# A hybrid decoder layer: the attention values as seven block products instead of two plain passes

## The chip, the cores and the metric

The kernel runs on one core of a Trainium2 chip. The metric is the device time of one execution in microseconds (us), as a median over runs. Engines are named TensorE (PE, with PEld for its weight loads), VectorE (DVE), ScalarE (ACT), GpSimd (POOL) and SyncE (SP); SP, ACT and POOL also issue DMA transfers, each from a queue of its own that runs in order.

## The reference

One decoder layer, float32, 512 tokens, width 1024:

```python
x = x + 0.5 * swiglu(rms_norm(x, norm_ffn1_w), ffn1_w_in, ffn1_w_out)
x = x + hybrid_mixer(rms_norm(x, norm_mix_w), w_in_mix, ..., rel_bias, w_out_mix, lambda_init)
x = x + memory_cross_attention(rms_norm(x, norm_cross_w), rms_norm(mem, norm_mem_w), ...)
x = x + 0.5 * swiglu(rms_norm(x, norm_ffn2_w), ffn2_w_in, ffn2_w_out)
return rms_norm(x, norm_final_w)

def hybrid_mixer(h, w_in, ...):
    z, xbc, dt_raw, q, k, v = split_sizes(h @ w_in, IN_SIZES)
    # state-space group: conv, silu, 16 heads in 4 groups, scan in chunks of 128 tokens,
    # gate by silu(z), group norm  ->  y_ssd
    # differential attention: 8 heads, two softmaxes a head,
    #   w = p[:, :, 0] - lam * p[:, :, 1];  o = w @ v;  norm by head  ->  y_attn
    return concatenate([y_ssd, y_attn], axis=-1) @ w_out
```

The change concerns `v = h @ w_in[:, 5136:6160]`, a product of 512 x 1024 by 1024 x 1024, and some steps that lie round it in time.

## The kernel before, in words

**Tiles.** Activations lie with features on the 128 partitions and the 512 tokens along the row: eight tiles `x[k]` of 128 x 512. Products in nearly full float32 precision are made of fast float32r matmuls: every operand is split into a high part (rounded by ScalarE, L155) and a low part (the rest, by VectorE, L156), and a product is three matmuls, high by high, high by low, low by high (`mm3`, L312). `load_w` (L172) brings a weight tile of 128 x 1024 from memory on SP's queue and splits it; six such tiles can be raw (`wr`), three split (`wh`, `wl`).

**Block products.** The feed-forwards use Winograd's form of Strassen's method: both operands are cut into 2 x 2 blocks, and seven products of sums of blocks replace eight products. `quad` (L257) does that with weights stationary and 256 tokens streaming; `out_blocks` (L1158) does it with activations stationary and 512 weight columns streaming ("by token"). Sums of activation blocks are made by VectorE (`sums_of`, L199: four sums of 256 columns, then a split into high and low); sums of weight blocks come from transfers that add into SBUF, issued on POOL's queue (`raw_w`, L243), from VectorE (L294, L297), or, for the second feed-forward, from sums that are made in DRAM ahead of time by `block_sums_in_dram` (L1138), a chain that issues one copy on SP and one adding transfer on POOL for each of some 46 tiles.

**Order.** `Order` (L57) writes the program down. Dense work (`od.add`) is a list of generators, taken one after the other; beside it run chains (`od.spawn`), each of which says after every step how many microseconds of TensorE time are to pass until its next one. `od.t` counts that time from the matmuls written so far. SP and POOL keep the written order. TensorE, VectorE and ScalarE get their order at compile time from a scheduler that goes by the written order and by its own estimate of when each instruction is ready, so that a later instruction can be put ahead of an earlier one. `behind(...)` (L184) forbids that for the instructions inside it: they come after the given instruction on the same engine.

**The stage round the change.** After the first feed-forward (`ffn1`, three thirds of block products and output tiles; its last output tile calls `fin1`, L533) the dense order is: memory keys, query and key of head 0, step sizes (`steps_dense`), `values(0)`, queries and keys 1 to 3, `group_dense(0)`, output of heads 0 to 3 (`out_attn`), `values(1)`, queries and keys 4 to 7, and so on. Beside them run these chains:

- `normed` (L401): the mix norm's row (`Stat.finish`, `row_of`), then eight normed and split tiles `h[k]`.
- `head(hd)` (L688): scores, softmaxes, transposes, product with the values of the head's half (`vs[hd // 4]`), norm.
- `group(g)` (L828): the scan of four state-space heads. For each of two pairs j, ScalarE makes the decays `rs` (L888 to L891) in tiles that were loaded from the `cum` values, VectorE masks them (L892), and TensorE makes `pf` (states by c, L895) and `py` (L900).
- `memory_norm` (L945): spawned beside the second third of `ffn1`, the sums of squares of the memory, a column of inverse roots (a power on POOL, L357), and its row: `row_of` (L360) puts the column on a diagonal (VectorE, L368), multiplies it with ones on TensorE (`nrow`), and ScalarE copies the row out (L396).

`values(hg)` (L663) computes 512 of the 1024 value columns: for each of four weight tiles, two feature tiles by four token blocks by three matmuls, 96 in all, into four PSUM banks, activations stationary; then four splits. Both calls together make 192 matmuls of 512 columns.

## Time and profile before

| | before |
|---|---|
| median of 3 runs | 1329.92 us (1329.41 to 1332.98) |
| the profiled execution | 1331.07 us |
| its span, first to last instruction | 1329.3 us |
| mean granted TensorE clock | 0.993 |
| ScalarE busy | 664.0 us (50%) |
| DMA | 222.71 MB, mean 168 GB/s |

How to read it: the profile comes from one execution. Busy times are shares of the span; matmuls overlap, so that the length of one is longer than the distance to the next. A row of the timeline gives start and length in us, engine, line, operation, output and inputs, their shapes, a count, and in brackets how long the engine had been idle and who ended that. A row of the windows gives a stretch, its length, and busy time and count for each engine, then the granted clock (1.00 is full), the share of the 16 DMA engines and GB/s.

### The profile page before, as it was taken

How to read it: one execution, taken by the hardware profiler on the slowest of the kernel's cores; microseconds unless marked ns; L12 is line 12 of the kernel's file. 1: busy time of each engine (PE TensorE's matmuls, PEld its weight loads, DVE VectorE, ACT ScalarE, POOL GpSimd, SP SyncE). 2: the span in 40 equal slices, each digit the busy share in tenths (PEclk: the TensorE clock that was granted, in tenths of full speed). 3: DMA queues.
4: the chain of work that ended last, by engine and by line, in shares of the span. 5: the costliest groups of instructions: out<-in, count | busy, mean ns of one | idle time of the engine just before them, and what ended most of it. 6: DMA issues, size and time to landing. Idle time of an engine off the chain costs nothing.

```text
span 1329.3 us, 20031 instructions
## 1 busy us (share of the span) xinstructions
PE 1309.1 (98%) x7769; PEld 1138.8 (86%) x7769; DVE 974.4 (73%) x1527; ACT 664.0 (50%) x1114; POOL 112.5 (8%) x127
## 2 busy tenths in 40 slices
PE   9999999999999999999999989999999999999997
PEld 7898998899887778877788878888889999989995
DVE  6874778477886586557867767656678878887886
ACT  6442445154554475436644645434465545554564
POOL 0000010000020111100112012020001100000001
PEclk9999999999999999999999989999999999999998
DMA  7435577546582723673366477775138976666762
GB/s 271 111 127 127 127 199 245 134 112 194 170 272 79 215 63 104 189 239 98 85 181 181 92 204 228 213 181 154 64 111 237 248 222 174 193 193 173 192 202 95
DMA packets 74143, 222.71 MB, mean 168 GB/s; under 512 B 8424, under 2 KB 20176, under 8 KB 73696
## 3 DMA queue, kind: packets, MB, share of 16 engines
q1 hardware_dynamic: 52400, 174.42, 39.4%
q0 software_dynamic: 11904, 40.45, 16.6%
q10 hardware_dynamic: 9744, 6.56, 2.5%
q8 instruction: 61, 1.00, 0.3%
q14 instruction: 34, 0.28, 0.1%
HBM read 219.24 MB, written 50.91 MB: 203 GB/s over the span
## 4 chain that ended last, share of the span: by engine, by line
PE 93%; DVE 3%; ACT 2%; DMA 1%; issue 1%; POOL 0%; POOLq 0%; ACTq 0%; DVEq 0%
PE qb L240 12%; PE po L146 10%; PE pm L146 10%; PE qe L240 8%; PE qa L240 8%; PE pxbc L146 7%; PE pcq L146 3%; PE pz L146 3%; PE pv L146 3%; PE ob L1185 3%; PE pq L146 3%; PE pk L146 2%; PE oa L1185 2%; PE oe L1185 2%; PE pa L146 2%; PE pcv L146 2%
## 5 line engine op out<-in xcount | busy, mean ns | idle before, releaser
L155 ACT ACTIVATE wh<-wr 128x1024 fp32r<-128x1024 f32 (+2 forms) x311 | 316.9, 1021 | 369.9 <-PE po L146 56.6
L156 DVE TENSOR_TENSOR wl<-wr,wh 128x1024 fp32r<-128x1024 f32 (+2 forms) x311 | 365.6, 1177 | 108.7 <-ACT wh L155 106.6
L146 PE MATMUL po<-gh,wh 128*128 128x512 f32 x176 | 68.8, 392 | 0.0
L146 PE MATMUL po<-gl,wh 128*128 128x512 f32 x176 | 68.5, 390 | 0.0
L146 PE MATMUL po<-gh,wl 128*128 128x512 f32 x176 | 68.4, 389 | 0.0
L240 PE MATMUL qa<-hml,wh 128*128 128x256 f32 x216 | 61.1, 283 | 0.0
L240 PE MATMUL qa<-hmh,wl 128*128 128x256 f32 x216 | 61.1, 283 | 0.0
L240 PE MATMUL qa<-hmh,wh 128*128 128x256 f32 x216 | 61.1, 283 | 0.0
L146 PE MATMUL pxbc<-hnh,wh 128*128 128x512 f32 x128 | 52.3, 409 | 0.0
L704 ACT ACTIVATE ec<-ec,mn 128x512 f32<-128x512 f32 (+3 forms) x64 | 35.4, 555 | 30.2 <-DVE mn L703 30.2
L146 PE MATMUL pxbc<-hnh,wl 128*128 128x512 f32 x128 | 50.4, 394 | 0.0
L146 PE MATMUL pxbc<-hnl,wh 128*128 128x512 f32 x128 | 50.2, 392 | 0.0
L240 PE MATMUL qe<-s31h,wh 128*128 128x256 f32 x152 | 43.9, 289 | 1.4 <-ACT wh L155 1.4
L240 PE MATMUL qe<-s31h,wl 128*128 128x256 f32 x152 | 43.9, 289 | 0.8 <-DVE wl L156 0.8
L510 DVE TENSOR_TENSOR upd<-po,row 128x512 f32<-128x512 f32 x24 | 16.6, 691 | 38.1 <-PE po L146 37.8
L240 PE MATMUL qe<-s31l,wh 128*128 128x256 f32 x152 | 43.7, 288 | 0.0
L240 PE MATMUL qb<-s24h,wl 128*128 128x256 f32 x152 | 43.0, 283 | 0.0
L240 PE MATMUL qe<-s24h,wh 128*128 128x256 f32 x152 | 43.0, 283 | 0.0
L240 PE MATMUL qe<-s24l,wh 128*128 128x256 f32 x152 | 43.0, 283 | 0.0
L240 PE MATMUL qe<-s24h,wl 128*128 128x256 f32 x152 | 43.0, 283 | 0.0
L240 PE MATMUL qb<-hmh,wh 128*128 128x256 f32 x152 | 43.0, 283 | 0.0
L240 PE MATMUL qb<-hml,wh 128*128 128x256 f32 x152 | 43.0, 283 | 0.0
(443 smaller groups left out, 4070.3 us busy)
## 6 DMA issues: line engine op xcount, KB each, us to landing
wr<-in_f2q SPq DMA_DIRECT2D x44, 512.0 KB, 4.4
wr<-in_f1q SPq DMA_DIRECT2D x40, 512.0 KB, 4.3
isum<-in_f2q SPq DMA_DIRECT2D x22, 512.0 KB, 5.5
wr<-isum SPq DMA_DIRECT2D x22, 512.0 KB, 4.3
wsum<-in_f2b SPq DMA_DIRECT2D x20, 512.0 KB, 7.9
wr<-wsum SPq DMA_DIRECT2D x20, 512.0 KB, 4.5
wr<-in_f1q POOLq DMA_DIRECT2D x16, 512.0 KB, 7.0
wr<-in_f1o SPq DMA_DIRECT2D x16, 512.0 KB, 4.3
```

The costliest lines, as they stand in the source:

```text
L146: nc.tensor.matmul(out, w, x, start=start, stop=stop)
L155: S.activation(hi, src, AF.Copy),
L156: V.tensor_tensor(lo, src, hi.bitcast(F32), ALU.subtract),
L240: nc.tensor.matmul(out, a_[:, wc], b_, start=first and f == 0 and kp == 0 and j == 0, stop=kp == n - 1 and j == 2, skip_group_check=True)
L510: V.tensor_tensor(upd, po, row4, ALU.mult)
L704: S.activation(ec[:, :n], ec[:, :n], AF.Exp, bias=mn, scale=-1.0, accum_out=sm[c][:, i : i + 1])
L1185: nc.tensor.matmul(ps, a_[:, ts], b_[:, ws], start=first and k == 0 and j == 0, stop=k == n - 1 and j == 2, skip_group_check=True)
```

## The change

- **Values.** `values()` is called once, where `values(0)` stood, and makes all 1024 columns by a new function `by_token`: the weights are regrouped on the host into four blocks (`wvb`, halves of the features' tile pairs by halves of the columns), and seven products of 4 tile pairs, 2 token blocks and 3 matmuls of 512 columns are made, 168 matmuls. Six banks of PSUM are used, two for each of three accumulators. Two of the weight sums (t, m7) come from adding transfers on POOL, two (t2, t4) from VectorE in place. `values(1)` is gone from its place behind `out_attn(0, ...)`.
- **Sums of h.** `normed` keeps the unsplit tiles and, after the eighth, makes the block sums of the four pairs, 2.4 us apart. The values wait for them in the written order.
- **Forced order.** The newest dense or chain matmul is remembered (`newest_mm`); the matmuls of `row_of`, and `pf` and `py` of a group, are put behind it. `pf` moves behind the wait before `py`, and the 2.0 us wait that stood ahead of the decays of pair 0 moves behind them.
- **Times.** Head 0 starts 38.1 us later in the written order (behind the values). `memory_norm` adds a tile every 1.25 us instead of 2.0 and makes its row 42 us after the sums instead of 6. `block_sums_in_dram` starts 60 us after the feed-forward instead of 10, with steps of 4.5 and 8.0 us instead of 5.0 and 9.0.

```diff
     def mm(out, w, x, start, stop):
         od.t += (1 if w.dtype == R32 else 4) * (x.free_size() + 8) / 2400
-        nc.tensor.matmul(out, w, x, start=start, stop=stop)
+        newest_mm[:] = [nc.tensor.matmul(out, w, x, start=start, stop=stop).ins]
...
+    def by_token(blocks, g, ps, done):
+        n = len(g)
+        parts = [(k, min(k + 2, n)) for k in range(0, n, 2)]
+        a_ps, e_ps, b_ps = ps
+
+        def bring(src, *more):
+            return [raw_w(*(b[:, lo * T : hi * T] for b in (src, *more)), n=(hi - lo) * T) for lo, hi in parts]
+
+        raws = {"m1": bring(blocks[B11]), "t": bring(blocks[B12], blocks[B11]), "m3": bring(blocks[B22])}
+        steps = [("m1", a_ps, "11"), ("t", e_ps, S1), ("t2", b_ps, S2), ("m7", b_ps, S3), ("m3", e_ps, S4), ("m2", a_ps, "12"), ("t4", b_ps, "22")]
+        steps = [(name, out, which, part) for name, out, which in steps for part in range(len(parts))]
+
+        def weights(name, part):
+            if part == 0 and name == "t":
+                raws.pop("m1")
+                raws["m7"] = bring(blocks[B12], blocks[B22])
+            elif part == 0 and name == "m3":
+                raws.pop("m7")
+                raws["m2"] = bring(blocks[B21])
+            if name in ("t2", "t4"):
+                raw = raws["t"][part]
+                V.tensor_tensor(raw, raw, raws["m3" if name == "t2" else "m2"][part], ALU.add)
+            else:
+                raw = raws[name][part]
+            return split_w(raw)
+
+        kept = []
+        w = weights("m1", 0)
+        for i, (name, out, which, part) in enumerate(steps):
+            (wh, wl), first = w, name in ("m1", "t")
+            if i + 1 < len(steps):
+                w = weights(steps[i + 1][0], steps[i + 1][3])
+            for t in range(2):
+                ts = slice(t * P, (t + 1) * P)
+                for k in range(*parts[part]):
+                    gh, gl = g[k][which]
+                    ws = slice((k - parts[part][0]) * T, (k - parts[part][0] + 1) * T)
+                    for j, (a_, b_) in enumerate(((gh, wh), (gl, wh), (gh, wl))):
+                        od.t += (T + 8) / 2400
+                        newest_mm[:] = [nc.tensor.matmul(out[t], a_[:, ts], b_[:, ws], start=first and k == 0 and j == 0, stop=k == n - 1 and j == 2, skip_group_check=True).ins]
+                    yield
+            if part < len(parts) - 1:
+                continue
+            if name == "m1":
+                for t in range(2):
+                    S.activation(b_ps[t], a_ps[t], AF.Copy)
+            elif name == "t":
+                for t in range(2):
+                    kept.append(s2("p5"))
+                    S.activation(kept[t], e_ps[t], AF.Copy)
+            elif name == "t2":
+                for t in range(2):
+                    u2 = s2("u2")
+                    S.activation(u2, b_ps[t], AF.Copy)
+                    V.tensor_tensor(e_ps[t], e_ps[t], u2, ALU.subtract)
+            elif name == "m7":
+                for t in range(2):
+                    V.tensor_tensor(kept[t], kept[t], b_ps[t], ALU.subtract)
+                    done[B22](t, kept[t])
+            else:
+                block = {"m3": B12, "m2": B11, "t4": B21}[name]
+                for t in range(2):
+                    done[block](t, out[t])
...
             eng.tensor_tensor(diag, ident[:, None, :].to_broadcast([P, nb, P]), c[:, :, None].to_broadcast([P, nb, P]), ALU.mult)
-            mm(pr, ones_r, diag.rearrange("p a b -> p (a b)"), j == 0, j == 1)
+            with behind(list(newest_mm)):
+                mm(pr, ones_r, diag.rearrange("p a b -> p (a b)"), j == 0, j == 1)
...
             if k > 0:
-                dst.append(split("hn", hf.pop(k - 1)))
+                dst.append(split("hn", hf[k - 1]))
                 yield 1.6
+        for k in range(0, KT, 2):
+            fe, fo = hf.pop(k), hf.pop(k + 1)
+            sums.append(of_halves(dst[k], dst[k + 1]) | sums_of(fe[:, :H], fe[:, H:], fo[:, H:], fo[:, :H]))
+            yield 2.4
...
-            od.spawn(block_sums_in_dram(), 10.0)
+            od.spawn(block_sums_in_dram(), 60.0)
...
-    def values(hg):
-        pv = [acc("pv") for _ in range(4)]
...
+    def values():
+        yield lambda: len(h_sums) == KT // 2
+        a_ps, e_ps, b_ps = [acc("va") for _ in range(2)], [aux("ve") for _ in range(2)], [acc("vb") for _ in range(2)]
+        tiles = [[None] * 4 for _ in range(2)]
+
+        def place(hg, half):
+            def done(t, src):
+                tiles[hg][2 * half + t] = split("v", src)
+            return done
+
+        done = {B11: place(0, 0), B12: place(1, 0), B21: place(0, 1), B22: place(1, 1)}
+        yield from by_token(a["wvb"], h_sums, (a_ps, e_ps, b_ps), done)
+        h_sums.clear()
+        vs.update(enumerate(tiles))
...
-        od.spawn(head(hd, q, kq, bias), W["h0"])
+        od.spawn(head(hd, q, kq, bias), W["h0"] if hd else W["h0"] + W["v"])
...
             st.append(sc)
-            yield W["gs"] if c < 2 else W["gt"]
+            if c < 2:
+                yield W["gs"]
...
                 V.tensor_tensor(r, r, cbm, ALU.mult)
+            yield W["gd"] + (W["gt"] if j == 0 else 0.0)
             pf = aux("pf")
-            for c in range(1, 4):
-                mm(pf[:, c * P : (c + 1) * P], st[c - 1][:, j * P : (j + 1) * P], ct[:, c * P : (c + 1) * P], True, True)
-            yield W["gd"]
-            for c in range(4):
-                for hh in range(2):
-                    pp = slice(64 * hh, 64 * hh + 64)
-                    mm(py[pp, c * P : (c + 1) * P], xdt[c // 2][:, c % 2, (2 * j + hh) * 64 : (2 * j + hh + 1) * 64], rs[hh][:, c], True, True)
+            with behind(list(newest_mm)):
+                for c in range(1, 4):
+                    mm(pf[:, c * P : (c + 1) * P], st[c - 1][:, j * P : (j + 1) * P], ct[:, c * P : (c + 1) * P], True, True)
+                for c in range(4):
+                    for hh in range(2):
+                        pp = slice(64 * hh, 64 * hh + 64)
+                        mm(py[pp, c * P : (c + 1) * P], xdt[c // 2][:, c % 2, (2 * j + hh) * 64 : (2 * j + hh + 1) * 64], rs[hh][:, c], True, True)
...
         for mk in mem:
-            yield 2.0
+            yield 1.25
             with behind(recent):
                 st_mem.add(mk)
         yield 3.0
-        yield from st_mem.finish(6.0)
+        yield from st_mem.finish(42.0)
...
-    od.add(values(0))
+    od.add(values())
...
-    od.add(values(1))
...
                 nc.sync.dma_start(jobs[n][0], jobs[n][1])
-                yield 5.0
+                yield 4.5
...
                 G.dma_start(to, more, accum_op=ALU.add, max_dma_last_dim=4 * D)
-                yield 9.0
+                yield 8.0
```

More of the change, by code (lines that the diff above doesn't have):

```diff
@@ L138, in dump @@
             nc.sync.dma_start(dbg[name], t.bitcast(F32) if t.dtype == R32 else t)
-    last, start, last_sum, recent, newest = [], [], [], [], []
+    last, start, last_sum, recent, newest, newest_mm = [], [], [], [], [], []
     V, S, G = nc.vector, nc.scalar, nc.gpsimd
@@ L239, in add_product, with raw_w @@
                     od.t += (H + 32) / 2400
-                    nc.tensor.matmul(out, a_[:, wc], b_, start=first and f == 0 and kp == 0 and j == 0, stop=kp == n - 1 and j == 2, skip_group_check=True)
+                    newest_mm[:] = [nc.tensor.matmul(out, a_[:, wc], b_, start=first and f == 0 and kp == 0 and j == 0, stop=kp == n - 1 and j == 2, skip_group_check=True).ins]
                 yield
-    def raw_w(src, *more):
-        raw = wp.tile([P, D], F32, tag="wr", name=nm("wr"), bufs=6)
+    def raw_w(src, *more, n=D):
+        raw = wp.tile([P, n], F32, tag="wr", name=nm("wr"), bufs=6)
         nc.sync.dma_start(raw, src)
@@ L251, in split_w @@
     def split_w(raw):
-        hi = wp.tile([P, D], R32, tag="wh", name=nm("wh"))
-        lo = wp.tile([P, D], R32, tag="wl", name=nm("wl"))
+        hi = wp.tile([P, raw.shape[1]], R32, tag="wh", name=nm("wh"))
+        lo = wp.tile([P, raw.shape[1]], R32, tag="wl", name=nm("wl"))
         newest[:] = [split_into(hi, lo, raw)[0].ins]
@@ L399, in make_h, with normed @@
         return split("hm", x[k], par[:, c + k : c + k + 1])
-    def normed(st, c, dst):
+    def normed(st, c, dst, sums):
         yield from st.finish()
@@ L523, in body @@
             st1.add(x[k])
-    st_mix, h = Stat(), []
+    st_mix, h, h_sums = Stat(), [], []
     def beside(ti):
@@ L661, in body @@
     vs = {}
-    def values(hg):
-        pv = [acc("pv") for _ in range(4)]
-        for kk in range(4):
-            w = load_w(a["wv"][hg, kk])
-            if kk < 3:
-                order = [(k2, tb) for k2 in range(2) for tb in range(4)]
-            else:
-                order = [(k2, tb) for tb in range(4) for k2 in range(2)]
-            for k2, tb in order:
-                k = 2 * kk + k2
-                mm3(pv[tb], h[k], w, k == 0, k == KT - 1, wc=slice(tb * P, (tb + 1) * P), xc=slice(k2 * T, (k2 + 1) * T))
-                yield
-        vs[hg] = [split("v", pv[tb]) for tb in range(4)]
+    def values():
[10 more added lines that the diff above has]
+        vs.update(enumerate(tiles))
     def queries_keys(hd):
@@ L1184, in some @@
                     od.t += (T + 8) / 2400
-                    nc.tensor.matmul(ps, a_[:, ts], b_[:, ws], start=first and k == 0 and j == 0, stop=k == n - 1 and j == 2, skip_group_check=True)
+                    newest_mm[:] = [nc.tensor.matmul(ps, a_[:, ts], b_[:, ws], start=first and k == 0 and j == 0, stop=k == n - 1 and j == 2, skip_group_check=True).ins]
                 yield
```

8 lines of the change are left out of this document (4 added, 4 removed).

## The prediction

> **What bounds the kernel now.** I read the page's busy times first, then the waits of TensorE, then the chain in order of time, and last the timeline round each wait.
>
> ```profile
> span 1329.3 us, 20031 instructions
> ## 1 busy us (share of the span) xinstructions
> PE 1309.1 (98%) x7769; PEld 1138.8 (86%) x7769; DVE 974.4 (73%) x1527; ACT 664.0 (50%) x1114; POOL 112.5 (8%) x127
> ```
>
> TensorE has work in all but 20 us of the span, so the end moves only with what TensorE has to do, with holes in its row, or with its clock. Its waits (total, times, longest) name the holes:
>
> ```profile
> PE py L146 <- DVE gate L892: 2.4, 1, 2.4
> PE pf L146 <- DVE st L876: 1.7, 2, 1.4
> PE qe L240 <- ACT wh L155: 1.4, 1, 1.4
> PE qe L240 <- DVE wl L156: 0.8, 1, 0.8
> ```
>
> Two places: the state products of a head group (pf, py), and a block product of the first feed-forward (qe). The change touches both, beside its main part.
>
> **Term 1: fewer matmuls.** The value products are three groups like this one (the other two take one low half each), 192 matmuls:
>
> ```profile
> L146 PE MATMUL pv<-wh,hnh x64: 389/389/507, 402.6 to 574.4; 128*128 128x512 f32 x64
> ```
>
> 389 ns is one with its drain. What one costs is the distance to the next, which the chain in order of time gives (start, length, count):
>
> ```profile
> 392.67 5.44 PE pk L146 x24
> ...
> 1006.27 2.88 PE qe L240 x24
> ...
> 1173.35 5.44 PE ob L1185 x24
> ```
>
> That is 0.2267 us for 512 columns and 0.12 for 256; the third row has the form of the new products (activations stationary, weights streaming). The new code has 7 products x 2 token blocks x 4 tile pairs x 3 = 168 matmuls, 24 fewer: **-5.4 us**. Nothing else on TensorE changes in number. The Trainium skill ("TensorE: Matmul & The Clock Gate", section "Back-to-back issue gap") gives about 131 ns as the sustained spacing at 512 columns; by that the term would be an estimated -3.1. The trace disagrees with 227 ns, and the measurement decides.
>
> **Term 2: what VectorE gets instead.** The stage runs from the mix norm to the end of the values, 362 to 441 us in the new order too (40 us up to the values, then 168 x 0.2267 = 38). Columns: length, busy time and count of PE, PEld, DVE, ACT, POOL, clock, DMA.
>
> ```profile
> 362.00:441.00 79.00, 78.31 (x458) 65.44 (x458) 55.87 (x113) 37.64 (x72) 11.67 (x11) 1.00 0.63 182
> ```
>
> ```profile
> L156 DVE TENSOR_TENSOR wl<-wr,wh 128x1024 fp32r<-128x1024 f32 x280 | 342.3, 1223 | 102.9 <-ACT wh L155 101.1 <-DMA isum<-in_f2q 0.5
> ```
>
> ```profile
> L206 DVE TENSOR_TENSOR s<-fe x8: 417/420/421, 41.6 to 991.0; 128x256 f32<-128x256 f32 x8
> ```
>
> ```profile
> L703 DVE CUSTOM_DVE_ANT_0 ec<-ps,bias 128x512 f32<-128x512 f32 (+3 forms) x8 | 3.6, 486 | 1.4 <-PE ps L146 1.4
> L156 DVE TENSOR_TENSOR vl<-pv,vh 128x512 fp32r<-128x512 f32 x4 | 2.7, 684 | 4.1 <-ACT vh L155 4.1
> L715 DVE SCALAR_TENSOR_TENSOR ec<-ec,rl,ec 128x512 f32<-128x512 f32 (+3 forms) x4 | 2.2, 546 | 0.0
> L156 DVE TENSOR_TENSOR wt<-pt,wt 128x128 fp32r<-128x128 f32 (+3 forms) x4 | 1.9, 486 | 2.3 <-ACT wt L155 2.3
> ```
>
> VectorE's bill for these 79 us: 55.9 as it was; less head 0, which now starts behind the values (3.6 + 2.2 + 1.9 = 7.7 in the rows shown, 402 to 441); plus ten weight splits (14 for the four of this stage) at 1.22, 12.2; plus four sums of weight tiles of the same shape, 4.9; plus the sums of h, 16 halves at 0.42 and 8 low parts at 0.68, 12.2; plus four low parts of v, 2.7; plus four subtractions from PSUM at about 0.68, 2.7. Together 82.9. Head 0's small operations are not taken off and lengths overlap a little, so I read it as 76 to 83: VectorE is full. What a nearly full VectorE does to TensorE shows in the second feed-forward, whose block products ask for a weight tile as often:
>
> ```profile
> 1020.00:1050.00 30.00, 30.00 (x252) 30.00 (x251) 26.76 (x34) 18.30 (x25) 5.06 (x6) 1.00 0.93 244
> ```
>
> At 89% TensorE loses nothing. 89% of 79 is 70; the excess is 6 to 13 us. Splits of the memory keys, the time-step chain and the low parts of v, q0 and k0 (a third of the bill or less) can slide past what TensorE waits for, and the fixed order on the engine decides whether they do. I take **+4 us**, nearer to 0 (all slides) than to 9 (the middle of 6 to 13, none slides). Likeliest late: the sums S1, wanted 5.4 us after the first product starts and queued behind eight normed tiles, and the weights of t2, which need a sum and a split.
>
> The product m7 goes into the PSUM bank that t2 has just filled, so ScalarE must have copied it first. TensorE has six matmuls on the other bank meanwhile, 1.36 us, and the copy costs 0.58:
>
> ```profile
> L299 ACT ACTIVATE u<-qb x19: 577/582/592, 83.3 to 1270.5; 128x512 f32<-128x512 f32 x19
> ```
>
> So 0, or up to 1 if a weight split stands in front of it on ScalarE. Edits with one answer: the weight sums by transfer land as they do in the first feed-forward,
>
> ```profile
> wr<-in_f1q POOLq DMA_DIRECT2D x16, 512.0 KB, 7.0
> ```
>
> 7 us behind a plain load, with three products (16 us) ahead of m7; hidden. If that cover went, two tiles would come up to 7 late. The DRAM sums share SP's and POOL's queues with them; they start 50 us later and so leave POOL free here, and their closer pacing (12.5 for 14 us, some 50 jobs) gives the 50 us back. Behind m7's sums on POOL stand the exponential of a_log and the store of cum, which the decays read; their first product comes about 100 us later:
>
> ```profile
> L146 PE MATMUL py<-gate,xdt x64: 272/273/473, 539.2 to 803.6; 128*64 128x128 f32 x64
> ```
>
> Head 0 then stands together with heads 1 to 3 as heads 4 to 7 do already, and the second values no longer stand between the output products and query 4. I put 0 for these, with -0.5 to +2 as ends.
>
> **Term 3: the memory norm's row.** ScalarE before the block product that waited, TensorE in the same stretch, and its window:
>
> ```profile
> 252.92 1.06 ACT L155 ACTIVATE wh<-wr 128x1024 fp32r<-128x1024 f32 x1 [4.40 <-PE po L146]
> 267.13 0.38 ACT L396 ACTIVATE row<-nrow 128x256 f32<-128x256 f32 x1 [13.15 <-PE nrow L146]
> 267.41 1.05 ACT L155 ACTIVATE wh<-wr 128x1024 fp32r<-128x1024 f32 x1
> ```
>
> ```profile
> 266.70 0.40 PE L146 MATMUL nrow<-ndiag,ones_r 128*128 128x256 f32 x2
> ...
> 274.00 0.28 PE L240 MATMUL qb<-s24h,wh 128*128 128x256 f32 x1
> ```
>
> ```profile
> 272.00:276.00 4.00, 4.00 (x28) 4.00 (x28) 3.72 (x4) 2.62 (x4) 0.00 (x0) 0.75 0.01 4
> ```
>
> ScalarE stood 13 us in front of `row`, the last step of the memory norm, with the split of the next weights (267.41) queued behind it. From 266.70 to 274.00 TensorE did two matmuls of the row and 24 of the product, 26 x 0.12 = 3.1 us of work in 7.3: 4.2 us lost, of which the waits above are 2.2 and the rest is the clock (0.75 in the last window). The change starts the sums of squares closer together (1.25 for 2 us a tile) and finishes 42 for 6 us after them: eight tiles save 6 us, the row moves 36 us later in the written order, net 30, out of the hand-over between output tiles and block products into the block products of the last third. The step issues one power on POOL, four small operations and two diagonals on VectorE, two matmuls and one copy; the keys need the row only after 389 us (the pk row above starts behind it). What is late there is the same handful of operations, now behind a VectorE with inputs long ready: up to 1 us. I take **-3.7**, ends -4.2 and +0.5.
>
> **Term 4: the forced order.** TensorE round the wait for the gate in group 3, then ScalarE, the clock, and the load of those weights (count, KB, us to landing):
>
> ```profile
> 784.53 0.59 PE L146 MATMUL pst<-xde,btk 128*128 128x256 f32 x2
> ...
> 791.49 0.77 PE L146 MATMUL pm<-yah,wh 128*128 128x512 f32 x1
> ...
> 796.52 0.40 PE L146 MATMUL pm<-yah,wh 128*128 128x512 f32 x1
> ```
>
> ```profile
> 790.43 0.61 ACT L155 ACTIVATE wh<-wr 128x512 fp32r<-128x512 f32 x1
> ```
>
> ```profile
> 790.00:792.00 2.00, 1.57 (x5) 1.22 (x6) 1.30 (x3) 2.00 (x6) 0.00 (x0) 0.50 1.02 416
> ```
>
> ```profile
> wr<-in_woa SPq DMA_DIRECT2D x2, 256.0 KB, 6.2
> ```
>
> In 12.0 us TensorE did twelve matmuls of 512 columns (2.7) and ten small ones (1.2 at 0.12): 8.1 lost, half the clock included. pf and one pair of py were put ahead of the output products that the code writes before them. Bound behind the newest dense matmul they no longer stop TensorE there; VectorE's `e` and `y` wait for them instead, some us later, and nothing dense waits for those until the last output projection. But look at what is late next: the weights of that same output product are split at 790.43, behind the group's exponentials, and TensorE could not have started at 784.5 without them. Landed they were sooner (6.2 us from an issue ahead of the hole). If ScalarE keeps its order, the start moves from 791.49 to 791.04 (790.43 + 0.61), 0.5 us; if the split goes first, all 8.1. The group's exponentials are written 2 us earlier after the change, which frees ScalarE about that much sooner, and the clock falls less. I take **-3.0**, nearer to the small end. For the other places where the row or pf is now bound (no wait there today beyond a few tenths) I put 0.
>
> **Sum.** -5.4 + 4 - 3.7 - 3.0 = -8.1. The profiled execution took 1331.07 (its span 1329.3 and 1.8 round it), 1.15 over the median 1329.92. 1331.1 - 8.1 = 1323.0; at the median 1321.8.
>
> **Rivals.** (a) *The order frees everything*: VectorE's excess half as costly, both stalls gone: -5.4 + 2 - 4.2 - 8.1 = -15.7, median 1314.2. For it: the splits wait only in ScalarE's queue, not for data. Against: ScalarE is busy all of 790 to 792 and the exponentials have to run some time. (b) *VectorE takes the gain*: -5.4 + 9 - 3.7 - 0.5 = -0.6, median 1329.3: no change. For it: 82.9 against 79. Against: a third can wait. Here the change would also not do what its last words say, since the forced order only swaps the wait for the gate for the wait for the weights. (c) *Slower*: the same shortage, but with the clock. Its place is the second to fourth value product, its price 9 us of stalls, and its point is a weight tile that is late by 1.4 to 2 us: as in term 3, where waits of 2.2 us brought another 2.0 through the clock, 9 of stalls bring about 8. -5.4 + 17 - 3.7 - 0.5 = +7.4, median 1337.3. Against it: stalls of one product give VectorE time for the next. The Trainium skill ("TensorE: Matmul & The Clock Gate", section "Why this matters for your kernels") asks only for no idle gaps over about 3 us, by which (c) would end as (b); the row of term 3 shows the clock down after shorter waits, so I keep (c).
>
> **Chances and range.** Forecast 0.47 (own range 1317 to 1326), (a) 0.20, (b) 0.21, (c) 0.12. A measurement of this kernel can tell about 0.3%, 4 us, from no change. Faster: all of (a), 0.45 of the forecast and 0.04 of (b), 0.69; the same: 0.02 and 0.17, 0.19; slower: (c), 0.12. The range 1312 to 1332 takes in (a), the forecast and (b), and leaves out (c) and the far ends of the small terms, under 2 in 10.
>
> **What would show it.** Right: 168 records in place of 192 for the values at the same spacing; VectorE busy over 90% in the stage, with waits of TensorE in the value products named after wl or the sums, 2 to 6 us in all; no wait of ScalarE for nrow ahead of the first block product of the last third; pf and py without waits, and `pm` in group 3 waiting for wh or wl instead. Wrong: TensorE whole through the values (term 2 is 0), the hole at 784 unchanged in length, a new hole over 3 us outside these places, or the clock at half in the values.

## The result and the profile after

| | before | after |
|---|---|---|
| median, 6 runs each | 1331.76 us | 1360.51 us (1358.50 to 1367.28) |
| ratio | | 1.0232 [1.0212, 1.0251] |
| the profiled execution, its span | 1331.07, 1329.3 | 1367.28, 1365.5 |

The change makes the kernel slower by 29 us. One execution of experiment 13 took 3332.76 us, far outside the others, and is left out of its median. From the page of after, the busy times, their share of the span and the instructions:

```profile
PE 1313.2 (96%) x7745; PEld 1138.7 (83%) x7745; DVE 998.0 (73%) x1565; ACT 676.1 (50%) x1134; POOL 117.2 (9%) x131
```

There are the 24 matmuls fewer (7745 for 7769), but TensorE's busy time has not fallen, since part of it runs at half clock, and 52 us of the span are holes where there were 20. The largest waits of TensorE (total, times, longest):

```profile
PE ve L356 <- ACT wh L155: 10.9, 1, 10.9
PE ps L146 <- DVE mn L778: 7.6, 3, 5.7
PE pdt L146 <- DVE ql L160: 7.6, 1, 7.6
PE pm L146 <- ACT wh L155: 7.0, 2, 5.7
```

Stretches of after (length; busy and count of PE, PEld, DVE, ACT, POOL; clock; DMA):

```profile
362.00:441.00 79.00, 65.08 (x365) 53.81 (x363) 60.49 (x104) 34.69 (x51) 12.28 (x11) 0.95 0.53 148
...
360.00:400.00 40.00, 35.08 (x244) 32.29 (x243) 36.31 (x57) 20.64 (x29) 9.36 (x8) 0.99 0.67 183
400.00:440.00 40.00, 32.01 (x137) 23.52 (x137) 26.15 (x51) 14.88 (x24) 2.93 (x4) 0.92 0.38 112
440.00:480.00 40.00, 29.61 (x116) 21.88 (x117) 19.28 (x32) 16.57 (x26) 0.00 (x0) 0.80 0.80 224
...
600.00:640.00 40.00, 34.34 (x154) 25.94 (x154) 20.10 (x51) 14.38 (x31) 8.22 (x7) 0.91 0.60 160
...
800.00:840.00 40.00, 34.34 (x168) 28.15 (x167) 28.35 (x47) 21.70 (x43) 7.36 (x7) 0.91 0.76 220
```

Forty minus the second figure is idle time of TensorE; a clock of 0.80 takes another fifth of what is busy. In the five rows of 40 us that is 34.6 idle and some 15 by the clock. In the stage that was read as full on VectorE (first row), VectorE was busy 60.5 of 79 us while TensorE lost 14. Four holes carry most of it.

**Hole 1, 395.5 to 403.1.** TensorE, and VectorE in the same time:

```profile
403.10 0.64 PE L146 MATMUL pdt<-hnh,wdts 128*32 128x512 f32 x1 [7.58 <-DVE ql L160]
```

```profile
395.37 0.42 DVE L206 TENSOR_TENSOR s<-hf 128x256 f32<-128x256 f32 x1
...
402.37 0.68 DVE L160 SCALAR_TENSOR_TENSOR ql<-pq,qh 128x512 fp32r<-128x512 f32 x1
```

and ScalarE:

```profile
401.09 0.63 ACT L155 ACTIVATE ck<-ckf 128x512 fp32r<-128x512 f32 x1 [2.31 <-DVE ckf L1052]
...
401.63 0.58 ACT L159 ACTIVATE qh<-pq 128x512 fp32r<-128x512 f32 x1
```

The step product `pdt` needs a PSUM bank; the four are taken by memory keys and by q and k of head 0, and q's bank comes free with its split. The last matmul of q started at 389.69. The low part of q stands on VectorE behind the new sums of h, and it needs the high part, which stands on ScalarE behind the high parts of the sums and behind `ck`, whose input VectorE made late for the same reason.

**Hole 2, 435.3 to 446.2.** TensorE, then ScalarE, whose rows ACTq are transfers that it issues:

```profile
446.19 0.79 PE L356 MATMUL ve<-wh,s24h 128*128 128x512 f32 x1 [10.90 <-ACT wh L155]
```

```profile
432.71 1.10 ACTq L900 DMA_DIRECT2D gate<-cum_d  x2
433.85 10.66 ACTq L900 DMA_DIRECT2D th<-cum_d  x2
444.56 0.63 ACT L155 ACTIVATE vh<-p 128x512 fp32r<-128x512 f32 x1 [16.23 <-issue]
445.10 1.04 ACT L155 ACTIVATE wh<-wr 128x1024 fp32r<-128x1024 f32 x1
```

ScalarE computed nothing for 16.23 us, with the split of the next value weights queued behind. For the first 4.4 of them it issued nothing either; the store of `cum`, which the loads read, was issued at 426.47 and landed 6.2 us later, just ahead of the first load. Then it stood 11.8 us at issuing the loads of the first group's decays, 10.66 of them for the last pair. What was on the way then in after, and below it the same loads in before (count, KB, us to landing):

```profile
isum<-in_f2q SPq DMA_DIRECT2D x5, 512.0 KB, 7.2
...
gate<-cum_d ACTq DMA_DIRECT2D x2, 256.0 KB, 18.3
th<-cum_d ACTq DMA_DIRECT2D x2, 256.0 KB, 26.6
wr<-in_wk SPq DMA_DIRECT2D x1, 512.0 KB, 19.3
cum_d<-ct_sb POOLq DMA_DIRECT2D x1, 32.0 KB, 6.2
```

```profile
gate<-cum_d ACTq DMA_DIRECT2D x2, 256.0 KB, 10.6
th<-cum_d ACTq DMA_DIRECT2D x2, 256.0 KB, 16.5
...
cum_d<-ct_sb POOLq DMA_DIRECT2D x1, 32.0 KB, 2.9
```

Before, the same issue of the last pair took 2.19 us and TensorE did not wait; now the decays fall into the middle of the value products and on top of the DRAM sums (`isum`). The key weights of head 1 land after 19.3 us (ScalarE stood 10.3 for them), and shorter waits, 1.75 us at most, follow behind the hole.

**Hole 3, 619 to 625:** `ps` of head 4 waits 5.7 us for VectorE, which waits for the head's bias from memory. The second value stage used to stand between. **Hole 4, 822 to 828,** in group 3 (TensorE, then ScalarE):

```profile
827.70 0.80 PE L146 MATMUL pm<-yah,wh 128*128 128x512 f32 x1 [5.66 <-ACT wh L155]
828.29 0.63 PE L146 MATMUL pm<-yal,wh 128*128 128x512 f32 x1
828.72 0.63 PE L146 MATMUL pm<-yah,wl 128*128 128x512 f32 x1
```

```profile
826.12 0.61 ACT L967 ACTIVATE gate<-gate 128x512 f32<-128x512 f32 x1
...
827.04 0.61 ACT L155 ACTIVATE wh<-wr 128x512 fp32r<-128x512 f32 x1
```

The waits of pf and py are gone, and that of `pm` for its weights, split behind the exponentials, is in their place. The distance of 0.43 us between the two rows behind the wait is the half clock.

### The profile page after: what moved, and what is told of

Its sections match the earlier page's. It is cut to its first block, busy times and chain, and to the rows that moved or that the text cites. A ratio compares the mean times of both kernels' runs of the same rounds, so it can differ in the third digit from the quotient of the medians.

```text
span 1365.5 us, 20091 instructions
## 1 busy us (share of the span) xinstructions
PE 1313.2 (96%) x7745; PEld 1138.7 (83%) x7745; DVE 998.0 (73%) x1565; ACT 676.1 (50%) x1134; POOL 117.2 (9%) x131
## 5 line engine op out<-in xcount | busy, mean ns | idle before, releaser
L155 ACT ACTIVATE wh<-wr 128x1024 fp32r<-128x1024 f32 (+2 forms) x317 | 322.9, 1021 | 374.8 <-PE po L146 61.7
L156 DVE TENSOR_TENSOR wl<-wr,wh 128x1024 fp32r<-128x1024 f32 (+2 forms) x317 | 372.3, 1177 | 115.8 <-ACT wh L155 113.1
L240 PE MATMUL qb<-s31h,wh 128*128 128x256 f32 x152 | 43.2, 284 | 0.8 <-ACT u L299 0.8
L240 PE MATMUL qb<-s24h,wh 128*128 128x256 f32 x152 | 43.0, 283 | 0.0
L240 PE MATMUL qb<-s31h,wl 128*128 128x256 f32 x152 | 43.0, 283 | 0.0
```

What stands on the lines that cost most here:

```text
L155: S.activation(hi, src, AF.Copy),
L156: V.tensor_tensor(lo, src, hi.bitcast(F32), ALU.subtract),
L240: newest_mm[:] = [nc.tensor.matmul(out, a_[:, wc], b_, start=first and f == 0 and kp == 0 and j == 0, stop=kp == n - 1 and j == 2, skip_gr ...
```

## The experiments

Ratios are to the kernel before, run on the same chip. The chip differs between groups of experiments (the kernel before took 1331.3 to 1332.3 us in median), and each interval is some 2 to 3 us to either side, so a difference of 1 or 2 us between two experiments shows nothing. Two theories stood at the start. *Queues*: hole 2 and what follows come from ScalarE and SP standing at transfers. *VectorE*: the stage simply has too much for VectorE, as term 2 had it. For hole 1 a third was put beside them, *bank*: it is only q's split that stands in the wrong place.

**1. DRAM sums later** (after)

```diff
-            od.spawn(block_sums_in_dram(), 60.0)
+            od.spawn(block_sums_in_dram(), 110.0)
```

> The kernel after, with the weight sums in DRAM begun at 110 us of the planner's clock in place of 60. Queue theory (the hole of 10.9 us at 435 to 446 us and the one at 462 to 468 us come from ScalarE and SP standing at the issue of loads that share the transfer queues with these sums): 12 to 16 us off the time after, the two holes under 2 us. Rival, ScalarE would stand at these loads anyway because they wait for the store of cum_d: 2 to 5 us off. VectorE theory (the added sums make VectorE late): no change, within 0.3%, since VectorE's work is the same.

1344.89 us, 1.0100 [1.0082, 1.0119]: 15.6 us off. ScalarE's rows and the landings:

```profile
431.19 1.19 ACTq L900 DMA_DIRECT2D th<-cum_d  x2
```

```profile
gate<-cum_d ACTq DMA_DIRECT2D x2, 256.0 KB, 10.5
th<-cum_d ACTq DMA_DIRECT2D x2, 256.0 KB, 14.8
```

With the DRAM sums out of the way the same issue takes 1.19 us for 10.66, the loads land as they did before, the store of `cum` lands after 3.3 us, and hole 2 is gone. VectorE's work is the same, so this half of the loss was not VectorE's.

**2. Decays from another queue** (after)

```diff
-            S.dma_start(r, bass.AP(cum_d.tensor, ...))
+            (S if g else G).dma_start(r, bass.AP(cum_d.tensor, ...))
```

> The kernel after, with the loads of cum_d for the decays of the first head group issued from POOL's queue, not ScalarE's; nothing is taken out. Queue theory: the hole of 10.9 us ahead of the value products' second weights at 446 us goes, with the half clock behind it: 12 to 16 us off the time after if nothing else is late there, 5 to 10 if the SP queue's part (the 4.2 us of idle time at 462 to 482 us) stays. VectorE theory: no change, within 0.3%.

1357.53 us, 1.0189 [1.0166, 1.0211]: only 3 us off. Hole 2 went, and a wait of 8.9 us of `ps` came at 459, since the query weights now landed late (ScalarE stood 11.0 us for them):

```profile
wr<-in_wq SPq DMA_DIRECT2D x3, 512.0 KB, 27.2
...
gate<-cum_d POOLq DMA_DIRECT2D x2, 256.0 KB, 14.3
th<-cum_d POOLq DMA_DIRECT2D x2, 256.0 KB, 24.3
```

So which queue issues is not what costs most of the time here. Experiment 1 won it back by taking other transfers out of the way; it is the transfers together that cost it. The Trainium skill ("DMA: Bandwidth & Descriptors", section "Issuing engines are not separate DMA queues") says that transfers of all issuing engines share the same 16 DMA engines and interleave there. These rows agree: another queue left the landings at 14 and 24 us, against 18 and 27.

**3. Sums of h 8 us later** (after)

```diff
+        yield 8.0
         for k in range(0, KT, 2):
             fe, fo = hf.pop(k), hf.pop(k + 1)
```

> The kernel after, with the sums of the normed halves (16 of VectorE's operations and their splits) put 8 us later in the planned order, behind q's split. Bank theory (the product pdt stands 7.6 us at 395.5 to 403.1 us for q's split, which frees its PSUM bank and is queued on VectorE behind these sums): this hole under 2 us and 5 to 8 us off, if the value products do not start later for it. VectorE theory in its plain form (the stage has too much work on VectorE, wherever it stands): the wait moves to the first value product and the time stays within 0.3%. Queue theory alone: no change.

1362.02 us, 1.0226 [1.0207, 1.0245]: nothing. Hole 1 closed, the values began 9.5 us sooner (398.7 for 408.2), and lost it again:

```profile
PE pdk L146 <- ACT dtf L686: 4.2, 1, 4.2
...
PE va L356 <- DVE ckf L1053: 1.1, 1, 1.1
```

The bank theory was too narrow: wherever the sums stand in the queue, something of that stretch stands behind them.

**4. The memory norm's times alone** (before)

```diff
-            yield 2.0
+            yield 1.25
...
-        yield from st_mem.finish(6.0)
+        yield from st_mem.finish(42.0)
```

> The kernel before with one part of the change alone: the statistics of the memory norm 1.25 apart in place of 2.0, and its row 42 in place of 6 behind. Term 3 of the prediction: 3 to 4 us off (0.2 to 0.3%), the two waits of the first memory products gone. Rival, the products find their next operand late anyway: 0 to 0.5 us.

1331.40 us, 0.9995 [0.9984, 1.0006]: nothing, and the row did not move at all:

```profile
267.24 0.38 ACT L396 ACTIVATE row<-nrow 128x256 f32<-128x256 f32 x1 [13.15 <-PE nrow L146]
```

The later written time alone does not move it; I take it that the compile-time order puts the row where its inputs are ready. With the forced order added:

**5. All of the forced order, nothing else** (before: `newest_mm`, `row_of`, pf and py behind it, the moved wait, and the norm's times, as in the change's diff)

> The kernel before with all of the forced order and nothing else: the memory norm's statistics and row as in the change, the row's products and group state products (pf, py) placed behind the newest matmul, the later step in the group. The order theory (the row leaves ScalarE's queue only with the forced order, which is what the run with the norm's times alone lacked; and in group 3 the wait for the gate is replaced by the wait of pm for its weights): 3 to 4 us off the time before, the hole at 264 to 274 us gone, the one at 784 to 796 us as long as it was (8 us). The prediction's terms 3 and 4: 6.7 off. Rival, the order frees both: 11 to 12 off. Rival, neither: 0.

1330.42 us, 0.9995 [0.9983, 1.0008].

```profile
269.56 0.39 PE L240 MATMUL qe<-s31h,wl 128*128 128x256 f32 x1 [0.48 <-DVE wl L156]
...
799.13 0.79 PE L146 MATMUL pm<-yah,wh 128*128 128x512 f32 x1 [5.66 <-ACT wh L155]
```

The hole at 264 to 274 went down to waits of 0.5; group 3 has the wait of after to the hundredth, with the half clock behind it, so nothing is won there. A wait of 2.64 us at 460 in a head's transposes is new; the profiled execution is the slowest of the twelve (1336.67 us). Together no gain that can be measured.

**6. DRAM sums at 60 alone** (before, with the change's three numbers)

> The kernel before with the weight sums in DRAM alone as in the change: begun at 60 in place of 10, 4.5 and 8 apart in place of 5 and 9. Queue theory in its plain form (these sums beside the loads of the first group's decays at 425 us make ScalarE and SP stand, wherever the value products are): 5 to 15 us more than before, a new hole between 425 and 470 us. Rival (it takes the new place of the value products, whose weights are split on ScalarE then; before, other weights are already split): within 0.3%.

1333.08 us, 1.0007 [0.9995, 1.0020]: the same, so the later start costs nothing by itself. And the reverse, **12. the main part alone** (after, with the forced order, the norm's times and the DRAM sums' times taken back):

> The kernel after with its side changes taken back: no forced order, the memory norm as before, the weight sums in DRAM begun at 10 and 5 and 9 apart as before. Left is the main part: value products of both halves at once, sums by transfers and VectorE, the second value stage gone from its place. Cover theory (the losses come from the main part and from what it uncovers; the sums begun at 60 add the collision with the first decays): 12 to 16 us over before if that collision needs the later start, 25 to 30 over if it comes anyway. The prediction's terms 1 and 2: 1.4 us under before.

1358.59 us, 1.0196 [1.0175, 1.0217]: 27 us over, as if the collision comes anyway. Begun at 10, the DRAM sums meet the decays just the same:

```profile
435.42 10.60 ACTq L899 DMA_DIRECT2D th<-cum_d  x2
446.06 0.63 ACT L155 ACTIVATE vh<-p 128x512 fp32r<-128x512 f32 x1 [15.27 <-issue]
```

The main part brings the loss; what the side changes add, 2 us, is within the noise. The collision does not need the later start, only sums that are still going at 430, and my first reading, that the move to 60 made it, is wrong.

**7. Sums of h on POOL** (experiment 1, with `V` replaced by `G` in the four operations of `sums_in_steps` for h)

> The kernel after with the weight sums in DRAM begun at 110 (1344.9 us measured), and with the block sums of the normed halves (16 additions and subtractions of 256 columns, 0.42 us each on VectorE, 6.7 us) on POOL. VectorE theory (the hole of 7.6 us at 395 to 403 us is VectorE's load between the norm and the values, so taking load off closes it and it does not come back later, as it did when the sums were only put later): 6 to 10 us less than 1344.9. Rival, the sums on POOL are slow (a 128x512 operation took 1.80 us there) and the value products wait for them instead: 0 or up to 5 us more.

1350.45 us, 1.0148 [1.0123, 1.0172]: 5.6 us slower than experiment 1, though the wait of `pdt` fell from 7.6 to 4.0. VectorE's groups from 372 to 402 us, here and then in experiment 1:

```profile
L156 DVE TENSOR_TENSOR wl<-wr,wh 128x1024 fp32r<-128x1024 f32 x7 | 10.7, 1522 | 0.0
L156 DVE TENSOR_TENSOR hnl<-hf,hnh 128x512 fp32r<-128x512 f32 x7 | 7.9, 1144 | 0.0
```

```profile
L156 DVE TENSOR_TENSOR wl<-wr,wh 128x1024 fp32r<-128x1024 f32 x7 | 8.6, 1222 | 0.4 <-ACT wh L155 0.4
L156 DVE TENSOR_TENSOR hnl<-hf,hnh 128x512 fp32r<-128x512 f32 x7 | 4.7, 685 | 0.0
```

While POOL adds, VectorE's operations of the same shape grow from 685 to 1144 ns: the load was moved and came back. The Trainium skill ("SBUF — State Buffer", section "SBUF: two separate sides") says that VectorE operations with two inputs in SBUF and GpSimd's lock each other out of a shared port pair. The trace agrees in that these operations, which have two inputs in SBUF, grew by 25 to 67%; the lock itself no row shows. So this run does not speak against the VectorE theory.

**8. Two covers put back** (experiment 1)

```diff
     od.add(group_dense(0))
+    od.add(queries_keys(4))
     od.add(out_attn(0, 0, 8))
-    for hd in range(4, 8):
+    for hd in range(5, 8):
...
+            if g == 3 and j == 1:
+                early["woa"] = load_w(a["woa"][1, SPLIT], 4 * P)
```

> The kernel after with the weight sums in DRAM begun at 110 (1344.9 us measured), with two covers put back: queries and keys of head 4 ahead of the first attention output products (so that the load of their bias, which VectorE stood 11.5 us for, has 18 us of products beside it), and the weights of the sixth output product of the second half (pm in group 3) loaded and split ahead of the last z product. Cover theory: the waits of ps (7.0) and of pm (5.7) go, each with the half clock behind it (2.5 to 4): 14 to 18 us less than 1344.9, which would be under the kernel before. If the next weights or the gate take the place of pm's wait: 6 to 10 less. Rival, VectorE's load is the limit there too: 0 to 3 less.

1339.34 us, 1.0067 [1.0043, 1.0092]: 5.6 off. Hole 3 is gone, hole 4 is not, its wait is still 5.66 us: with the first of three weights split early, the third still stands behind the exponentials.

**9 and 10. Head 1 ahead of the values, sums of h later** (both on experiment 1; 9 has also the covers of 8, with all three output weights ahead)

```diff
+        yield 8.0
         for k in range(0, KT, 2):
...
+    od.add(queries_keys(1))
     od.add(values())
-    for hd in range(1, 4):
+    for hd in range(2, 4):
```

> The kernel after with all covers: weight sums in DRAM begun at 110; queries and keys of head 4 ahead of the first attention output products; queries and keys of head 1 ahead of the value products, and the block sums of the normed halves 8 us later, behind q's split; the weights of the last three output products of the second half all loaded ahead of the first of them. Cover theory (every loss of the change is a wait for something that older work used to stand beside): against the 1339.3 us with two of these covers, the hole of pdt goes with its half clock (10 to 12 us), and so does the one of pm (6 to 8): 1319 to 1324 us, under the kernel before by 0.5 to 0.9%. Rival (VectorE's load sets the stretch from the norm to the end of the values; the waits come back in other places, as when the sums were only put later): 1333 to 1337, not under it.

> The kernel after with the weight sums in DRAM begun at 110 (1344.9 us measured), the block sums of the normed halves 8 us later, and queries and keys of head 1 (11 us of products with little for VectorE) ahead of the value products. Cover theory: the hole of 7.6 us at pdt, the half clock behind it and the stalls of the first value products all go: 10 to 12 us less than 1344.9. Rival, VectorE's load: the waits come back in the value products, 0 to 3 less.

1350.21 us, 1.0138 [1.0117, 1.0160], and 1355.27 us, 1.0178 [1.0159, 1.0197]: both worse than experiment 1. Hole 1 is gone, but one of 13 us opens inside the value products. SP, TensorE and VectorE of experiment 10:

```profile
407.75 43.33 SPq L246 DMA_DIRECT2D wr<-in_wvb  x3
```

```profile
450.78 0.79 PE L356 MATMUL vb<-wl,s31h 128*128 128x512 f32 x1 [13.32 <-DVE wl L156]
```

```profile
447.17 1.23 DVE L338 TENSOR_TENSOR wr<-wr,wr 128x1024 f32<-128x1024 f32 x1 [16.30 <-DMA wr<-in_wvb]
```

SP stood 43 us at three loads of value weights. The products hold raw tiles for long (`t` from its load to the last product), six is all there are, and head 1's weights had taken their turn. Here the cover costs more than the hole did; how the six were handed round was not followed up.

**11. Output weights ahead** (experiment 5, with the three loads ahead of the first product)

> The kernel before with all of the forced order (1330.4 us measured) and the weights of the last three attention output products loaded and split ahead of the first of them. Theory (in group 3 the forced order moved the wait from the gate to the weights of pm, whose split stands behind the group's exponentials on ScalarE): the hole of 5.7 us and the half clock behind it go, 7 to 8 us less than 1330.4. Rival, the wait for the gate comes back in its place: 0 to 3 less.

1329.24 us, 0.9982 [0.9970, 0.9993]: 1.2 under experiment 5, which is within the noise, where 7 to 8 were expected. The next product in the order now waits for its weights in the same place, 3.8 us.

**13, 14, 15. The sums left out** (experiment 1 without the sums of h, without those of the value weights, without both)

> The kernel after with the weight sums in DRAM begun at 110 (1344.9 us measured), and without the block sums of the normed halves: the products take plain blocks in their place, so 16 additions of 256 columns (0.42 us each), 8 splits of 512 (0.69) on VectorE and 8 on ScalarE are left out. VectorE theory (the hole of 7.6 us at pdt and the half clock behind it are VectorE's load of these 12 us): 10 to 13 us less than 1344.9. Rival, the hole is the order of PSUM banks and of the value weights: 0 to 3 less.

> The kernel after with the weight sums in DRAM begun at 110 (1344.9 us measured), and without the sums of the value weights: the four adding transfers on POOL and the four additions of 1024 columns on VectorE (1.21 us each) are left out; the raw blocks are held as long as before. If they are hidden, as the prediction put it: within 0.3% of 1344.9. If they hold VectorE or POOL up: 3 to 6 less.

> Both left out, the block sums of the normed halves and the sums of the value weights (weight sums in DRAM begun at 110): the new product order without the work that it adds to VectorE. VectorE theory: 12 to 17 us less than 1344.9, the stretch from 360 to 480 us as whole on TensorE as in the kernel before, and 1328 to 1333 in all, since the holes of the bias (7.0) and of pm (5.7) stay. Rival, order and transfers: 0 to 4 less.

1335.85 us, 1.0036 [1.0023, 1.0049]; 1343.09 us, 1.0089 [1.0072, 1.0105]; 1335.34 us, 1.0030 [1.0017, 1.0043]. From 362 to 441 us in experiment 1, then in 13:

```profile
362.00:441.00 79.00, 70.82 (x383) 58.09 (x382) 66.88 (x111) 40.28 (x60) 10.47 (x9) 0.94 0.49 130
```

```profile
362.00:441.00 79.00, 78.34 (x429) 65.67 (x430) 59.90 (x92) 39.04 (x55) 10.37 (x9) 1.00 0.61 157
```

Without the sums of h TensorE is whole, about 8.5 us are gained (by the ratios), and here they do not come back. VectorE's busy time differs by 7 us of 79 and has room in both, over the whole stage. It has little in the part of it where the sums stand: from 360 to 400 us it is busy 36.31 us in after (the row above), where TensorE loses 5, and in experiment 13

```profile
360.00:400.00 40.00, 39.56 (x263) 34.94 (x262) 33.32 (x46) 20.34 (x28) 9.02 (x8) 1.00 0.68 181
```

From 377 to 404 us it is busy 25.3 of 27 us in after, 22.2 before and 20.5 in experiment 13. Leaving out the sums takes work off ScalarE too, eight high parts of some 0.6 us. The weight sums cost 1.8 us or less in the medians, which these runs cannot tell from nothing: hidden, as predicted.

**16. Covers without head 1** (experiment 8, all three output weights ahead, sums of h 8 us later)

> The kernel after with the weight sums in DRAM begun at 110, queries and keys of head 4 ahead of the first attention output products, the block sums of the normed halves 8 us later, and the last three attention output weights loaded ahead; head 1 stays behind the value products, so that its weights do not stand between theirs. Against 1339.3 with the first two: 3 to 8 less for the hole of pdt, 3 to 4 for the one of pm: 1327 to 1333, about the kernel before. If the stalls of the first value products cost what the hole did, as in the run with the sums 8 us later: 1335 to 1338.

1338.12 us, 1.0051 [1.0037, 1.0066]. The stalls of experiment 3 are all there (`pdk` 4.2, `va` 1.1). No version with the change's main part reached the kernel before.

**17. One more split ahead** (experiment 11, without the change's main part)

```diff
+            if (hg, o) == (1, SPLIT):
+                early["wcv"] = load_w(a["wcv"][0])
...
-            w = load_w(a["wcv"][k])
+            w = load_w(a["wcv"][k]) if k else early.pop("wcv")
```

> The kernel before with all of the forced order and the last three attention output weights ahead (1329.2 us measured, where the first memory value product waited 3.8 us for its weights, split on ScalarE behind the exponentials of the group), and now those weights split ahead too, behind the first of the three products. If the splits are what is late: the wait and the half clock behind it go, 4 to 6 us less than 1329.2. Rival, the next thing behind the same exponentials (the memory tiles hm, split from 791.5 us on) is late by nearly as much: 0 to 3 less.

1325.53 us, 0.9963 [0.9950, 0.9977]: 0.37% under the kernel before, so it beats both kernels. It is 3.7 us under experiment 11, on another chip, with intervals that just meet.

```profile
788.94 0.50 PE L146 MATMUL pcv<-wh,hm 128*128 128x512 f32 x1 [2.03 <-ACT hm L159]
```

The rival's wait (hm) is there, but 2.03 us long and without the half clock.

## Why the prediction was wrong

**Term 1 was right.** 168 records, 0.227 us apart where nothing waits (24 distances from 453.29 to 458.73, 5.44 us).

**Term 2 is the step that failed,** in two ways. First, its reading: VectorE's bill against the length of the stage, 82.9 of 79, of which an excess would be lost. The bill was too long. In experiment 13 the values end inside the stage with TensorE whole, and VectorE is busy 59.9 us; with the 12.2 for the sums of h that makes 72.1. Ten more weight splits were counted, and there are six (22 for 16 before). The reading was also too coarse. Over the 79 us VectorE had room (60 to 67 busy), and yet the sums of h cost 8.5 us (experiment 13), because they fall between 377 and 404 us, ahead of q's split, where VectorE was nearly full (25.3 of 27 us). A block of 12 us on VectorE and 5 on ScalarE, engines whose order is fixed at compile time, stands there in front of q's split, the key factors, the step sizes and the first value weights, each of which holds up TensorE. Shifting the block (3, 16) only changed who stood behind it. Whether it is the amount of work in these 27 us or its order that costs the time, the runs do not separate: experiment 13 takes both away. The second feed-forward, whole at 89%, was no guide: VectorE makes sums between its weight splits there as well, so a share of that height does not tell by itself whether TensorE will wait.

Second, the "edits with one answer" that were put at 0. Of the DRAM sums the text said "they start 50 us later and so leave POOL free here", and of the decays' loads "their first product comes about 100 us later". I costed the DRAM sums by POOL's queue and the decays by who reads them, and neither by the other transfers on the way nor by the engine that stands at the issue. The two met while ScalarE had value weights to split, and it stood 16 us (experiment 1: 15.6 us, the largest term of all). The issuing engine is only where this shows first: with the issue on POOL's queue, ScalarE waited for query weights instead and 3 us were won (experiment 2). "The second values no longer stand between the output products and query 4" was written down and priced at 0; it was the cover of head 4's bias, 5.6 us (experiment 8).

**Term 3** had the mechanism half right. The hole at 264 goes, but not by the later time alone (experiment 4); it takes the bound order (experiment 5; the bound order without the later time was not run). Its 3.7 us are not found again in the time of experiment 5, and a new wait of 2.64 us with half clock behind it stands against them in its profile.

**Term 4** was -3.0 and came out as 0. The text named what would be late next, the weights split behind the exponentials, and then took 3.0 of the 8.1 all the same. Experiments 11 and 17 show why that row of waits is long: output weights, memory value weights, memory tiles, all behind the same 5 us or so of ScalarE. With the output weights split ahead the wait was 3.8 us, with both kinds 2.03 and no half clock.

**The rival (c)** had the sign, +7.4, and one of the causes with another place: before the value products, not inside them. What it lacked are the transfers, 15.6 us, and the bias, 5.6. Of the signs that were named, `pm` waiting for `wh` in group 3 came as said. VectorE over 90% in the stage did not, hole 2 stands in the value products for another cause than the sums, and holes 1 and 3 opened outside the places named.

The terms: 27 for the main part is -5.4 (matmuls), +15.6 (transfers), +5.6 (bias), +8.5 (sums of h), together 24.3 (with each run set against the kernel before on its own chip 16.1, 5.0 and 8.4, together 24.1); some 3 us are not placed, and the sum holds only if the parts add, which was not tried in one kernel. Why an issue takes 10.66 us in one state of the queues and 1.19 in another, the profile does not say.

## What to carry to other kernels

Cost a moved or uncovered transfer by who reads it, by what else is on the way at that time, and by what stands behind it on the engine that issues it. A share of busy time over a long stage does not tell whether an engine can take a block of new work; look at the part where the block stands, and list what stands behind the block in its order and who waits for each. Where one engine's queue makes a wait, write down the whole line behind it before counting a gain for its first member.

## What the runs showed of the hardware

- Half clock behind a wait of TensorE. In the twelve places of these traces with a wait of 2.2 to 4.4 us inside the run, the granted clock was 0.50 to 0.62 two to four us later. Below that the length alone does not tell: 2.03 us (experiment 17) left it at 1.00, and one and the same wait of 1.53 us, at 509 in experiments 9 and 10, was followed by 1.00 in the one and by half clock in the other (0.71 from 509 to 513). What else decides, no run here shows. Behind 2.64 us (experiment 5), where the matmuls came 0.43 us apart, and behind 2.03:

```profile
460.00:464.00 4.00, 3.74 (x10) 2.97 (x11) 3.63 (x13) 2.28 (x8) 0.00 (x0) 0.50 0.47 125
```

```profile
789.00:793.00 4.00, 4.00 (x17) 2.99 (x18) 3.70 (x7) 4.00 (x8) 0.00 (x0) 1.00 0.99 270
```

- Additions on POOL of 256 columns took 1.2 to 1.3 us in the mean (0.42 on VectorE) and lengthened VectorE's operations beside them by 25 to 67% (experiment 7: 1222 to 1522 ns, 685 to 1144 ns).
- The loads that spread values of `cum` over 128 partitions, 256 KB, landed after 10 to 27 us. Plain loads of 512 KB in the same stretch of after took 7.2 (`isum`) and 19.3 (`wk`), so how much of it is the form of the load and how much the traffic is not shown.
- The issue of two such loads kept ScalarE 10.66 us in after, 2.19 before and 1.19 in experiment 1.
